# Three padding tiles in a two-layer encoder kernel: every fp32r operand of TensorE moves to a multiple of 128 bytes

## The chip, the cores and the metric

The kernel is one program for one core of a Trainium2 chip. The metric is device time in microseconds (us): the median of several executions, lower is better.

## What is computed

The reference is a trunk of two encoder layers over 1,024 tokens of 1,024 channels, in float32:

```
for l in range(2):
    h = rmsnorm(x) * (1 + sc1) + sh1
    proj = h @ w_in[l]                       # 1024 -> 5792 columns
    ya = latent attention(cq, ckv, kr)       # 8 heads, keys of 64 + 32 rope
    yb = pooling branch(pu); yc = gated convolution branch(cx, cb, cc)
    merged = sigmoid gates of (ya, yb, yc)
    x = x + g1 * (merged @ w_out[l])
    h2 = rmsnorm(x) * (1 + sc2) + sh2
    x = x + g2 * expert_choice_moe(h2)       # 16 experts, 128 tokens each, 1024 -> 1024 -> 1024
return rmsnorm(x)
```

## The kernel before

Every large product is worked out three times over. An operand is split in a high part (`hi`, rounded to the fp32r type) and a rest (`lo`), by ScalarE and VectorE in `split` (L110), and TensorE adds hi by hi, hi by lo and lo by hi (`mm3`, L320):

```
for i, (a, b) in enumerate(((w_hi, h_hi), (w_hi, h_lo), (w_lo, h_hi))):
    for q in range(n):
        s = slice(512 * q, 512 * q + 512)
        PE.matmul(dst[:, s], a, b[:, s], start=start and i == 0, stop=stop and i == 2)
```

In each matmul the first operand (`a`, 128 columns) is loaded into the array as weights, and the second (`b`, mostly 512 columns) streams through it; below they are the loaded and the streamed operand. Every matmul has a weight load of its own.

A layer runs through these stages, in the order of the program, with nothing that reorders it:

- the projections: `hhi`/`hlo` (the normalised input, transposed) stream past columns of weights `whi`/`wlo`. In between `yhi`/`ylo` stream past the convolution's output weights, and the sums of the modulation are taken. The first block is done by quarters of 256 columns (L485).
- attention: queries (`cqhi`/`cqlo` past `qw`), scores (`khi`/`klo` past a tile named `raw`, which holds the queries), softmax on VectorE and ScalarE, transposes (L859), and the values (L867, L869, 256 columns).
- merge (`ohi`/`olo`) and output projection (L1137, 256 columns, `rg` and `whi`/`wlo` past `rg`), with the router behind it.
- the experts: the 128 rows of an expert, transposed (`T00`, `T01`, `T10`, `T11`), are loaded, and the weights `whi`/`wlo` of 512 columns stream. SyncE fetches 1 MB pieces of the weights ahead into 16 buffers (L1035); ScalarE and VectorE split each piece; TensorE multiplies it.
- in the first layer, the last expert's rows are added by TensorE at the start of the second (L1512: `T10`/`T11` stream past a selection matrix that lies in a tile named `xg`).

Tiles lie in pools that are stacked from the left and from the right end of the scratch memory in the order in which they are opened, so where a tile begins follows from the sizes of all that were opened before it on its side:

```
consts = ctx.enter_context(tc.tile_pool(name="consts", bufs=1, side="left"))
small = ctx.enter_context(tc.tile_pool(name="small", bufs=4, side="left"))
self.pool = self.stack.enter_context(pool("W", bufs=2, side="left"))
Hp = hs.enter_context(pool("H", side="right"))
r = [ep.tile([128, 8, 128], F32R, name=f"T{e % 2}{i}", bufs=1) for i in range(2)]
```

Of the kernel before, what the change touches and what calls it, by code (L numbers as in the profile page):

```python
# [9 lines left out]
F32 = mybir.dt.float32  # L10
# [28 lines left out]
# chunks of the modulation worked out in turn between the projections of a layer  # L39
# [15 lines left out]
def encoder(ctx, tc, x, c, positions, w_mod, b_mod, norm1_g, w_in, b_gate, q_norm_g, w_uq, kv_norm_g,  # L55
# [17 lines left out]
    dram = ctx.enter_context(tc.tile_pool(name="scratch", bufs=1, space=DR))  # L73
    pstate = {}

    def psum_open(n2, n1):
        """n2 tiles of two banks, n1 of one"""
        if "stack" in pstate:
            pstate["stack"].close()
        pstate["stack"] = ExitStack()  # L80
        pstate["pool"] = pstate["stack"].enter_context(pool("psum", space=PS))
        pstate["n"] = (n2, n1)
# [7 lines left out]
    class Weights:  # L90
        """tiles of the weights: as loaded, and in two parts"""
# [8 lines left out]

    W = Weights()
# [10 lines left out]
    def behind(*ins):  # L112
        """what follows comes after these on their engines"""
        st = ExitStack()
        for i in ins:
            st.enter_context(tc.issue_after(i.ins))
        return st

    def gated(ins, by):
        """ins waits for by"""  # L120
        tc.add_manual_dep(ins.ins, by.ins.name, mybir.DependencyInfo(mybir.DependencyClass.Sync, mybir.DependencyReason.DATA),
                          reason="order")

    # ---------------------------------------------------------------- scratch in DRAM
# [10 lines left out]
    # ---------------------------------------------------------------- constants  # L135
# [26 lines left out]
    # row k, column p: one where k < p  # L162
# [15 lines left out]
    # every token's number in two parts, and its affinities in three  # L178
# [12 lines left out]
    # ---------------------------------------------------------------- modulation rows  # L191
# [7 lines left out]
    def mod_first(j, P_, crep, onec):  # L199
        """the same by the tensor engine alone, four parts of the sum side by side"""  # L200
        raw = mod_load(0, j, P_, 2 if P_ is W else 3)
        if j % 2 == 0:
            pend["pm"] = ps1()
        pm = pend["pm"]
        o = 256 * (j % 2)
        for k in range(8):
            g = k % 4
            PE.matmul(pm[32 * g:32 * g + 32, o:o + 256], crep[:, k, :], raw[:, k, :], start=(k < 4), stop=(k >= 4),
                      tile_position=(0, 32 * g))
        if j % 2 == 1:  # L210
            mp = pend["pool"].tile([128, 512], F32, name="mp", bufs=1)
            ACT.copy(mp, pm)
            pr = ps1()
            for i in range(4):
                PE.matmul(pr[:, i:i + 1], mp[:, 128 * i:128 * i + 128], onec, start=True, stop=True)
            DVE.tensor_copy(modT[:, 2 * (j - 1):2 * (j - 1) + 4], pr[:, 0:4])

    def mod_chunk(l, j):
        """256 of the modulation's columns: the sum over k on the vector engine; mod_sum() follows later"""
        raw = mod_load(l, j, W, 2)  # L220
        acc = pend["pool"].tile([128, 256], F32, name="macc", bufs=9)
        DVE.tensor_scalar(acc, raw[:, 0], csil[:, 0:1], None, op0=OP.mult)
        for k in range(1, 8):
            DVE.scalar_tensor_tensor(acc, raw[:, k], csil[:, k:k + 1], acc, op0=OP.mult, op1=OP.add)
        mod_sums.append((l, j, acc))

    def mod_sum(pending=0):
        """the sums over the partitions of four such chunks, side by side"""
# [14 lines left out]
    # chunks of the rows: sh1 0-3, sc1 4-7, g1 8-11, sh2 12-15, sc2 16-19, g2 20-23  # L243
# [51 lines left out]
    # ---------------------------------------------------------------- helpers  # L295
# [9 lines left out]
    def load_split(src, kt, cols, raw_eng=None):  # L305
        """[128, kt, cols] block of weights, split in two parts."""
        raw = W.tile([128, kt, cols], F32, name="raw", tag="raw")
        SP.dma_start(raw, src)
        hi = W.tile([128, kt, cols], F32R, name="whi", tag="whi")
        lo = W.tile([128, kt, cols], F32R, name="wlo", tag="wlo")  # L310
        split(hi, lo, raw)
        return hi, lo

    def mm3(dst, w_hi, w_lo, h_hi, h_lo, start, stop):
        """dst[:, half] += w.T @ h for both halves of 512 columns, w: [K,128], h: [K,1024]"""
# [6 lines left out]
    for l in range(DEPTH):  # L322
        x_in = x.rearrange("b s d -> (b s) d") if l == 0 else xres[l - 1]

        # ------------------------------------------------------------ vectors of the layer
# [15 lines left out]
        # ------------------------------------------------------------ h, transposed, in two parts  # L341
# [23 lines left out]
        def block():  # L365
            """the next block of weights; the one after it is fetched meanwhile"""
            fetch()
            return ready.pop(0)
# [19 lines left out]
        if l == 0:  # L388
            psum_open(2, 4)
            with pool("xt", side="right") as xp:  # L390
# [9 lines left out]
                def hx_half(t, hf):  # L400
                    """half of the rows' columns, transposed"""
# [75 lines left out]
        def proj_quarters(dsts, w):  # L477
            """two column blocks, a quarter of the tokens after the other"""
# [21 lines left out]
        # ------------------------------------------------------------ gated convolution branch  # L500
# [66 lines left out]
        # ------------------------------------------------------------ pooling branch  # L567
# [63 lines left out]
        # ------------------------------------------------------------ gains of the norms  # L631
        def gain(pp, i, l_):
            """one plus the scale, times the norm's weights, as rows of 128"""
# [8 lines left out]
        # ------------------------------------------------------------ low-rank queries, keys and values  # L642
# [13 lines left out]
        with pool("cqt", side="left") as cp:  # L656
# [38 lines left out]
            # rope part of the keys: columns and the same columns with their halves swapped, both parts side by side  # L695
# [27 lines left out]
            def prepare(pp):  # L723
                # the router's weights with the norm's gain in them, and what the shift adds to its logits
# [23 lines left out]
            for dp in range(4):  # L748
                wg = block()
                for d in (2 * dp, 2 * dp + 1):  # L750
# [7 lines left out]
                    # w_out with the gate g1 of the residual in it  # L758
# [13 lines left out]
        # ------------------------------------------------------------ attention  # L772
        with pool("att", side="right") as ap:
# [27 lines left out]
            def k_pair(hp):  # L801
                """keys of two heads, and the query weights of both"""
# [60 lines left out]
            def av(h, g, phi, plo, po):  # L863
                """two query tiles, g = 0..3; po is [128, 512] for two g"""
# [85 lines left out]
        # ------------------------------------------------------------ merge and output projection  # L950
# [6 lines left out]
        # gated sum, transposed: [half of the tokens][part][half of the channels]  # L957
# [14 lines left out]
        def wout_load(q):  # L972
            """a quarter of w_out's columns, with the gate g1 of the residual in it"""
# [41 lines left out]
        def slot(s_):  # L1015
            """a buffer of two rows of k of an expert's weights"""
            p_, tag, bufs = s_
            return p_.tile([128, 2, 1024], F32, name="rg", tag=tag, bufs=bufs)
# [9 lines left out]
        def prefetch(n, by=None):  # L1028
            for _ in range(n):
                if chunks:  # L1030
                    w, e, j = chunks.pop(0)
                    # the last ones leave the buffers outside the ring to the rows of x
# [8 lines left out]
        with pool("wout", side="left") as op_:  # L1041
# [4 lines left out]
            # the 128 largest so far, the ranks of each eight reversed, and a copy for the steps of the merge  # L1046
# [8 lines left out]
            def top_round(i, r):  # L1055
                """eight more of a list's sorted 128 largest, in blocks from the last"""
# [5 lines left out]
            def merged(i):  # L1062
                """a list's largest into the largest so far"""
# [7 lines left out]
            def sort_steps(src, d0, d1, steps, rev):  # L1071
                """the steps of a merge, to d0 and d1 in turn"""
# [11 lines left out]
            def copied(t, dst, src):  # L1084
                """the last tile's copies stay off the scalar engine, which is busy then"""
                (ACT.copy if t < 7 else DVE.tensor_copy)(dst, src)

            def quick_sort(t):
                """a tile's affinities, sorted by 32 in four places, of which two with the sign turned"""
# [25 lines left out]
            def quick_list(t):  # L1115
                """the four merged: from the smallest by eights; the very last tile's stay unsorted by twos"""
# [75 lines left out]
            def h2_rows(t):  # L1192
                """the normalised rows, to be gathered by the experts"""
# [90 lines left out]
            # the 128th largest of every expert, on all partitions  # L1284
# [8 lines left out]
            # the tokens above it and those equal to it, each counted in their order  # L1293
# [22 lines left out]
        # ------------------------------------------------------------ experts  # L1316
# [3 lines left out]
        if True:  # L1320
# [40 lines left out]

            hot, idx, val, pick = {}, {}, {}, {}
            choose_last, gathers = [None], []

            def choose(e):
                """a one in the row of a token and the column of its slot"""
# [10 lines left out]
            def chosen(e):  # L1377
                """token and affinity of every slot"""
# [47 lines left out]
            for e in range(E):  # L1426
# [13 lines left out]
                if e + 2 == E:  # L1440
                    if not last:
                        # the first weights of the next layer
                        pend["w0"] = ring.tile([128, 8, 256], F32, name="rg", tag="rg", bufs=N_RING)
                        SP.dma_start(pend["w0"], cols(w_in[l + 1], O_CX, 256))
                    # the last expert's rows are added on chip
# [4 lines left out]
                    if last:  # L1450
                        # their rows as they are before it
# [11 lines left out]
                    # what the next norm multiplies by and adds  # L1463
# [6 lines left out]
            if last:  # L1470
                # the rows without the last expert's, then its rows over them
# [34 lines left out]
            def last_rows(t, xt, sel, ys):  # L1506
                """the last expert's rows onto 128 tokens"""
# [47 lines left out]
```

## Time and profile before

| | |
|---|---|
| three runs | 3419.47, 3422.6, 3423.29 us; median 3422.6 |
| span of the profiled execution | 3420.4 us (first to last instruction; its time outside the span is not listed) |
| TensorE busy | 3232.3 us, 94% of the span, 16,593 matmuls |
| VectorE, ScalarE, GpSimd busy | 2443.6, 1856.7, 384.1 us |
| mean granted clock of TensorE | 0.973 |
| moved by DMA | 686 MB, 201 GB/s |

A busy share is an average over stages with different limits, and matmuls overlap in the records: one that streams 512 columns is listed at some 395 ns, while the next one starts about 230 ns after it. So times between starts are what count, and the timeline shows them: a row of the timeline joins neighbouring instructions of one kind, and from the start of one row to the start of a later one, divided by the matmuls in between, is the time that one matmul takes up.

### The profile page before, as it was taken

The numbers are of one execution on the slowest core, as the hardware profiler recorded it, in microseconds if no ns is written. First come the engines' busy times: TensorE is split into PE (matmuls) and PEld (weight loads), VectorE is DVE, ScalarE is ACT, GpSimd is POOL, SyncE is SP. The second block draws the span as 40 slices with busy tenths as digits, with TensorE's granted clock in tenths as the row PEclk, the third lists the DMA queues.
The fourth block names the chain that finished last, engine by engine and source line by source line (L and its number), as shares of the span: only waits on it lengthen the run. The fifth ranks groups of instructions, "written<-read, shape, count | busy, mean of one in ns | idle before, by whom it ended". The sixth has DMA issues, their size and how long they took to land.

```text
span 3420.4 us, 43057 instructions
## 1 busy us (share of the span) xinstructions
PE 3232.3 (94%) x16593; PEld 2670.8 (78%) x16593; DVE 2443.6 (71%) x3730; ACT 1856.7 (54%) x2535; POOL 384.1 (11%) x364
## 2 busy tenths in 40 slices
PE   6999999999978799999989999999999869999996
PEld 5787787788878688888778887777887868888875
DVE  5555525499848899999864345347997488999997
ACT  5111213488734788887631121226885348888876
POOL 2001011000034101001020000010001330101010
PEclk8999999999989899999999999999999879999998
DMA  6346334100355899999622344340004559999994
GB/s 219 117 148 206 109 122 132 64 17 7 129 189 203 300 390 381 387 390 371 246 61 78 131 156 136 101 160 24 14 34 160 202 188 356 380 388 378 392 377 180
DMA packets 283373, 686.00 MB, mean 201 GB/s; under 512 B 24934, under 2 KB 139840, under 8 KB 283168
## 3 DMA queue, kind: packets, MB, share of 16 engines
q1 hardware_dynamic: 247008, 563.13, 44.4%
q0 software_dynamic: 33856, 111.74, 10.3%
q10 hardware_dynamic: 2304, 8.39, 0.7%
q8 instruction: 130, 2.13, 0.3%
q14 instruction: 75, 0.61, 0.1%
HBM read 607.63 MB, written 75.55 MB: 200 GB/s over the span
## 4 chain that ended last, share of the span: by engine, by line
PE 77%; DVE 12%; ACT 4%; DMA 3%; issue 2%; POOL 1%; SPq 0%; POOLq 0%; ACTq 0%; DVEq 0%
PE ps L320 63%; PE pa L1137 3%; DVE wlo L110 3%; PE pa L320 3%; DVE mx L841 2%; PE pa L859 2%; PE ps L1346 1%; DMA gh<-gate 1%; PE pa L867 1%; PE pa L869 1%; ACT pexp L846 1%; ACT whi L110 1%; DVE af L1060 1%; DVE top L1058 1%; PE pa L1178 1%
## 5 line engine op out<-in xcount | busy, mean ns | idle before, releaser
L110 DVE TENSOR_TENSOR wlo<-rg,whi 128x1024 fp32r<-128x1024 f32 x768 | 899.8, 1220 | 99.7 <-ACT whi L110 96.8
L110 ACT CAST whi<-rg 128x1024 fp32r<-128x1024 f32 x768 | 762.1, 1045 | 184.3 <-PE ps L320 184.2
L320 PE MATMUL ps<-whi,T 128*128 128x512 f32 x3072 | 846.9, 395 | 4.5 <-DVE T L110 2.3
L320 PEld LDWEIGHTS ps<-whi,T 128*128 128x128 f32 x3072 | 575.3, 189 | 130.5 <-DVE T L110 3.2
L320 PE MATMUL ps<-wlo,T 128*128 128x512 f32 x1536 | 490.7, 401 | 4.5 <-DVE wlo L110 2.5
L320 PE MATMUL ps<-hhi,whi 128*128 128x512 f32 x1376 | 437.1, 399 | 0.0
L320 PE MATMUL ps<-hlo,whi 128*128 128x512 f32 x1376 | 433.9, 396 | 0.0
L320 PE MATMUL ps<-hhi,wlo 128*128 128x512 f32 x1376 | 433.9, 396 | 0.0
L320 PEld LDWEIGHTS ps<-wlo,T 128*128 128x128 f32 x1536 | 281.1, 189 | 71.9 <-DVE wlo L110 14.6
L110 ACT CAST whi<-raw 128x2048 fp32r<-128x2048 f32 (+2 forms) x59 | 101.0, 1713 | 430.5 <-PE ps L320 409.2
L320 PEld LDWEIGHTS ps<-hhi,whi 128*128 128x128 f32 x1376 | 257.7, 188 | 67.6 <-issue 4.2
L320 PEld LDWEIGHTS ps<-hhi,wlo 128*128 128x128 f32 x1376 | 259.2, 188 | 63.2
L320 PEld LDWEIGHTS ps<-hlo,whi 128*128 128x128 f32 x1376 | 259.1, 188 | 63.1
L1137 PE MATMUL pa<-rg 128*128 128x256 f32 x768 | 189.4, 301 | 30.0 <-DVE rg L110 13.9
L110 DVE TENSOR_TENSOR wlo<-raw,whi 128x2048 fp32r<-128x2048 f32 (+2 forms) x59 | 121.0, 2051 | 107.9 <-ACT whi L110 107.9
L320 PE MATMUL ps<-khi,raw 128*128 128x512 f32 x512 | 167.2, 407 | 7.0 <-ACT pexp L846 5.7
L1137 PEld LDWEIGHTS pa<-rg 128*128 128x128 f32 x768 | 146.2, 203 | 33.2 <-DVE rg L110 15.0
L110 DVE TENSOR_TENSOR wlo<-pa,whi 128x512 fp32r<-128x512 f32 x256 | 169.5, 681 | 1.3 <-ACT whi L110 1.0
L1437 POOL DMA_INDIRECT xres<-y,idx x30 | 72.3, 2411 | 780.8 <-DVE y L1436 780.8
L846 ACT ACTIVATE pexp<-ps,nm 128x1024 f32<-128x1024 f32 x128 | 143.1, 1118 | 29.7 <-DVE nm L843 26.7
L841 DVE TENSOR_REDUCE mx<-ps 128x1 f32<-128x1024 f32 x128 | 155.1, 1213 | 5.5 <-PE ps L320 4.5
L110 ACT CAST whi<-pa 128x512 fp32r<-128x512 f32 x256 | 139.6, 588 | 8.4 <-PE pa L859 7.5
(409 smaller groups left out, 4894.8 us busy)
## 6 DMA issues: line engine op xcount, KB each, us to landing
rg<-in_w_gate_dram SPq DMA_DIRECT2D x128, 1024.0 KB, 9.3
rg<-in_w_up_dram SPq DMA_DIRECT2D x128, 1024.0 KB, 7.1
rg<-in_w_down_dram SPq DMA_DIRECT2D x128, 1024.0 KB, 7.9
raw<-in_w_mod_dram SPq DMA_DIRECT2D x48, 1024.0 KB, 5.4
raw<-in_w_in_dram SPq DMA_DIRECT2D x43, 1024.0 KB, 5.2
part<-pr POOLq DMA_DIRECT2D x32, 512.0 KB, 3.7
pr<-part POOLq DMA_DIRECT2D x16, 512.0 KB, 4.4
sq<-in_w_out_dram POOLq DMA_DIRECT2D x16, 512.0 KB, 4.5
```

Source lines behind the costliest of these rows:

```text
L110: return ACT.copy(hi, src), DVE.tensor_sub(lo, src, f(hi))
L320: PE.matmul(dst[:, s], a, b[:, s], start=start and i == 0, stop=stop and i == 2)
L841: DVE.reduce_max(mx, p, axis=AX.X)
L846: ACT.activation(e, p, AF.Exp, bias=nm, scale=SCALE, accum_out=sm)
L859: PE.transpose(p[:, 128 * k:128 * k + 128], e[:, o:o + 128], ident)
L867: PE.matmul(po[:, o:o + 256], vt[:, k, h, :], phi[:, k, :], start=(k == 0), stop=False, skip_group_check=True)
L869: PE.matmul(po[0:64, o:o + 256], vt[:, k, h, 0:64], plo[:, k, :], start=False, stop=(k == 7), skip_group_check=True)
L1058: DVE.max(v[:, 15 - r, :], a)
L1060: DVE.match_replace(a, v[:, 15 - r, :], a, -1.0)
L1137: PE.matmul(p[q // 2][:, 256 * (q % 2):256 * (q % 2) + 256], a, wos[q][b][:, k, :], skip_group_check=True, start=(k == 0 and i == 0 and q ...
L1178: PE.matmul(pls[t][:, :E], hT[:, 128 * k:128 * k + 128], wra[:, kk, :], start=(kk == 0), stop=(kk == 7))
L1437: POOL.indirect_dma_start(out=xres[l], in_=y, in_offset=None, compute_op=OP.add, out_offset=bass.IndirectOffsetOnAxis(ap=idx[e][:, 0:1], a ...
```

## The change

Three small tiles that nothing reads or writes are put in: 96 bytes per partition at the right end, 64 bytes on the left behind the constants, and 64 bytes in the pool of the experts, ahead of the `T` tiles. All other lines of the difference are comments.

```
@@ -71,10 +71,13 @@
     small = ctx.enter_context(tc.tile_pool(name="small", bufs=4, side="left"))
     dram = ctx.enter_context(tc.tile_pool(name="scratch", bufs=1, space=DR))
+
+    edge = ctx.enter_context(tc.tile_pool(name="edge", bufs=1, side="right"))
+    edge.tile([128, 24], F32, name="edge")
     pstate = {}
...
+    edge = ctx.enter_context(tc.tile_pool(name="edge2", bufs=1, side="left"))
+    edge.tile([128, 16], F32, name="edge2")
     W = Weights()
     W.open()
...
             hot, idx, val, pick = {}, {}, {}, {}
+            ep.tile([128, 16], F32, name="phase")
             choose_last, gathers = [None], []
```

No instruction is added, removed or moved: the lists of the five engines are the same row for row, with the same waits, 9,513 rows on TensorE's. What differs is where operands begin. In bytes past a multiple of 128, from the two built programs, for the 13,888 matmuls with fp32r operands:

| matmuls | streamed, loaded operand | columns | number | before (streamed, loaded) | after |
|---|---|---|---|---|---|
| projections, L320 | `hhi`/`hlo`, `whi`/`wlo` | 512 | 4,128 | 96, 64 | 0, 0 |
| keys' rope part, L705 | `hhi`/`hlo`, `rk` | 512 | 64 | 96, 64 | 0, 0 |
| first block, L485 | `hhi`/`hlo`, `whi`/`wlo` | 256 | 384 | 96, 64 | 0, 0 |
| scores, L320 | `khi`/`klo`, `raw` | 512 | 768 | 96, 64 | 0, 0 |
| queries, L320 | `cqhi`/`cqlo`, `qw` | 512 | 288 | 64, 96 | 0, 0 |
| values, L867 and L869 | `whi`/`wlo`, `vt` | 256 | 1,024 | 64, 96 | 0, 0 |
| output projection, L1137 | `rg`, `rg` | 256 | 768 | 96, 96 | 0, 0 |
| output projection, L1137 | `whi`/`wlo`, `rg` | 256 | 768 | 64, 96 | 0, 0 |
| experts, L320 | `whi`/`wlo`, `T00` to `T11` | 512 | 4,608 | 64, 0 | 0, 0 |
| `y`, `o`, `m` and `ck` products, L320 | `yhi`, `ohi`, `mhi`, `ckhi`, ... | 512 | 1,056 | 64, 64 | 0, 0 |
| last expert's rows, L1512 | `T10`/`T11`, `xg` | 512 | 32 | 0, 0 | 0, 0 |

The matmuls with plain float32 operands (transposes, sums) mostly move to 0 too; 64 of the 128 at the start (L208) have their loaded operand `crep` moved from 64 to 96.

## Rows read from the trace of the kernel before

**Rows 1.** The page: the chain that ended last, by engine and by line.

```profile
PE 77%; DVE 12%; ACT 4%; DMA 3%; issue 2%; POOL 1%; SPq 0%; POOLq 0%; ACTq 0%; DVEq 0%
PE ps L320 63%; PE pa L1137 3%; DVE wlo L110 3%; PE pa L320 3%; DVE mx L841 2%; PE pa L859 2%; PE ps L1346 1%; DMA gh<-gate 1%; PE pa L867 1%; PE pa L869 1%; ACT pexp L846 1%; ACT whi L110 1%; DVE af L1060 1%; DVE top L1058 1%; PE pa L1178 1%
```

**Rows 2.** Windows: length, busy PE, PEld, DVE, ACT, POOL; clock, DMA share, GB/s.

```profile
80.00:600.00 520.00, 520.00 (x2249) 412.71 (x2249) 266.95 (x357) 107.81 (x86) 41.80 (x78) 1.00 0.43 140
640.00:900.00 260.00, 253.83 (x1555) 217.96 (x1555) 237.66 (x469) 215.86 (x396) 1.60 (x3) 1.00 0.07 25
...
1150.00:1660.00 510.00, 508.54 (x2394) 411.64 (x2393) 470.90 (x445) 421.07 (x504) 48.96 (x28) 1.00 1.02 380
```

**Rows 3.** Timeline of TensorE in the projections (start, length; 26th row is last).

```profile
570.61 0.64 PE L320 MATMUL ps<-hhi,whi 128*128 128x512 f32 x2
...
582.33 0.63 PE L320 MATMUL ps<-hlo,whi 128*128 128x512 f32 x2
```

**Rows 4.** Timeline in the convolution's output product (22nd row is last).

```profile
251.44 0.61 PE L320 MATMUL ps<-yhi,wlo 128*128 128x512 f32 x2
...
260.96 0.61 PE L320 MATMUL ps<-yhi,wlo 128*128 128x512 f32 x2
```

**Rows 5.** Timeline in the last product of layer one's experts (7th row is last).

```profile
1704.81 1.07 PE L320 MATMUL ps<-whi,T 128*128 128x512 f32 x4
...
1708.93 1.07 PE L320 MATMUL ps<-whi,T 128*128 128x512 f32 x4
```

**Rows 6.** Timeline where the last expert's rows are added, four matmuls and what follows.

```profile
1728.89 1.07 PE L1512 MATMUL pa<-T,xg 128*128 128x512 f32 x4
1729.80 0.60 PE L385 MATMUL pa<-ident,xn 128*128 128x128 f32 x4
```

**Rows 7.** Timeline in the queries' product (11th row is last).

```profile
712.76 0.40 PE L320 MATMUL pa<-cqlo,qw 128*128 128x512 f32 x1
...
716.26 0.40 PE L320 MATMUL pa<-cqlo,qw 128*128 128x512 f32 x1
```

**Rows 8.** Groups of matmuls by operands: count, busy us, mean ns.

```profile
L320 PE MATMUL ps<-whi,T 128*128 128x512 f32 x3072 | 846.9, 395 | 4.5 <-DVE T L110 2.3 <-ACT T L110 2.2
...
L320 PE MATMUL ps<-hhi,whi 128*128 128x512 f32 x1376 | 437.1, 399 | 0.0
...
L320 PE MATMUL ps<-khi,raw 128*128 128x512 f32 x512 | 167.2, 407 | 7.0 <-ACT pexp L846 5.7 <-ACT raw L110 1.3
...
L320 PE MATMUL pa<-cqhi,qw 128*128 128x512 f32 x192 | 62.8, 394 | 3.0 <-ACT qw L110 3.0
```

**Rows 9.** Chain of attention in layer one (690 to 900 us), by line.

```profile
by line: PE ps L320 15.9%; PE pa L320 15.7%; DVE mx L841 12.7%; PE pa L859 10.9%; DVE wlo L110 8.0%; PE pa L867 7.1%; PE pa L869 6.8%; ACT pexp L846 6.1%; DVE pexp L849 3.6%; ACT whi L110 2.1%; DVE op L879 1.9%; DVE raw L110 1.7%; ACT ohi L
```

**Rows 10.** Timeline in the output projection (16th row is last).

```profile
1047.29 0.29 PE L1137 MATMUL pa<-rg 128*128 128x256 f32 x1
...
1049.08 0.28 PE L1137 MATMUL pa<-whi,rg 128*128 128x256 f32 x1
```

**Rows 11.** Timeline in the values (13th row is last).

```profile
688.73 0.28 PE L869 MATMUL pa<-wlo,vt 128*64 128x256 f32 x1
...
690.13 0.28 PE L869 MATMUL pa<-wlo,vt 128*64 128x256 f32 x1
```

**Rows 12.** Waits in the experts (1300 to 1600 us): total, times, longest.

```profile
ACT whi L110 <- PE ps L320: 41.2, 57, 1.2
```

**Rows 13.** Waits of SyncE's queue in the experts (1150 to 1710 us).

```profile
SPq L1035 <- DVE wlo L110: 378.4, 145, 5.2
```

**Rows 14.** Timeline of four matmuls of L1512 at half clock, and what follows.

```profile
1741.27 1.91 PE L1512 MATMUL pa<-T,xg 128*128 128x512 f32 x4
1742.98 0.41 PE L385 MATMUL pa<-ident,xn 128*128 128x128 f32 x1
```

**Rows 15.** Two stretches of L1512: the clock granted (PEclk).

```profile
1741.30:1742.90 1.60, 1.60 (x5) 1.19 (x5) 1.28 (x3) 1.54 (x4) 0.32 (x1) 0.50 0.04 15
1728.90:1729.80 0.90, 0.90 (x6) 0.69 (x5) 0.90 (x3) 0.87 (x2) 0.11 (x1) 1.00 0.00 0
```

More of the change, by code (lines that the diff above doesn't have):

```diff
@@ L73, in encoder @@
     dram = ctx.enter_context(tc.tile_pool(name="scratch", bufs=1, space=DR))
+    edge = ctx.enter_context(tc.tile_pool(name="edge", bufs=1, side="right"))
+    edge.tile([128, 24], F32, name="edge")
     pstate = {}
@@ L99, in close @@
             self.stack.close()
+    edge = ctx.enter_context(tc.tile_pool(name="edge2", bufs=1, side="left"))
+    edge.tile([128, 16], F32, name="edge2")
     W = Weights()
@@ L1362, in encoder @@
             hot, idx, val, pick = {}, {}, {}, {}
+            ep.tile([128, 16], F32, name="phase")
             choose_last, gathers = [None], []
```

## The prediction

> **What bounds the kernel now.** I read the page first, then the busy times of three stretches, the chain of waits, and last the timeline of TensorE. TensorE holds 77% of the chain that ends last, and the line of the split products, L320, 63% of the whole span [rows 1]. In the projections TensorE is busy without a gap, VectorE for 267 of 520 us; in the experts TensorE for 508.5 of 510 us, VectorE for 470.9; only in attention are TensorE (253.8 of 260) and VectorE (237.7) close to each other [rows 2]. In the experts ScalarE waits for TensorE to give a buffer back [rows 12], and the queue that fetches the weights waits for buffers too, 378 us in all [rows 13]; so neither the splits nor the loads hold TensorE up there. A matmul that takes up less time therefore shortens projections and experts one for one.
>
> The next question is how long a matmul takes up, from start to start, and whether that goes with where its operands begin (the offsets are those of the table in the change; here as streamed, loaded). The projections (96, 64): from 570.61 to 582.33 lie 25 rows of two matmuls, 11.72 us / 50 = **234.4 ns** [rows 3]. The convolution's output (64, 64), same line of code, same 512 columns, same stage: 21 rows of two, 9.52 us / 42 = **226.7 ns** [rows 4]. The experts (64, 0): 18 matmuls in 4.12 us, **228.9 ns** [rows 5]. The queries (64, 96): 15 in 3.50 us, **233.3 ns** [rows 7]. So the two kinds with a 96 in them stand near 234, the two without at 227 to 229. One small group already has what the change gives to all, (0, 0): the rows of the last expert, four matmuls at full clock [rows 15] from 1728.89 to the next row at 1729.80, 0.91 us / 4 = **227.5 ns** [rows 6]. That is the floor of (64, 64), on few samples.
>
> What else could make the difference? Not the load of the other engines: the 226.7 and the 234.4 stand in the same stage, with VectorE half idle [rows 2]. Not the clock, which is full in all of these stretches [rows 2]. What is left is the offset, or something else about the place of the tiles that goes with it.
>
> **The change part by part.** It issues nothing and moves nothing, so no wait, queue or DMA is added; the three tiles cost space alone. Each term is a number of matmuls by the difference of two such times.
>
> 1. *Projections and the keys' rope part*, 4,128 + 64 matmuls of (96, 64); the 4,128 are three groups of 1,376 [rows 8]. From 234.4 to 226.7 ns: 4,192 x 7.7 = **32.3 us**, all on the path, since TensorE has no gap there.
> 2. *Experts*, 3,072 [rows 8] and half as many with `wlo`, 4,608 of (64, 0). From 228.9 to 226.7: 4,608 x 2.2 = **10.1 us**, on the path. VectorE is the cover that could run out: it is busy for 470.9 of 510 us, so there are 39 us to take from TensorE in a layer before it leads, and the term takes 5.
> 3. *Scores and queries in attention*: 512 [rows 8] and half as many with `klo`, 768 of (96, 64), for which I take the projections' step, 768 x 7.7 = 5.9 us; 192 [rows 8] and half as many with `cqlo`, 288 of (64, 96), 288 x 6.6 = 1.9 us. Together 7.8, of which I count TensorE's share of the chain there, 15.9 + 15.7 + 10.9 + 7.1 + 6.8 = 56% [rows 9]: **4.4 us**. VectorE and ScalarE, late next, keep the rest.
> 4. *Matmuls of 256 columns*: 1,536 in the output projection at 1.79 us / 15 = 119.3 ns [rows 10], 1,024 in the values at 1.40 us / 12 = 116.7 [rows 11], 384 at the start (taken at 119 too). No row shows one at (0, 0). From below, half of a full-rate 512 (next paragraph), 106.7 ns: 2,944 x some 11.5 = 34 us, about half on the path, so 17. From above, the highest of these classes, 119.3, for the values too: 1,024 x 2.6 = 2.7 us lost. They are far apart, and the rows themselves hardly differ between offsets, so I take **0**.
> 5. *The 1,056 of (64, 64) and 32 of (0, 0)*: at the floor already, **0**. The float32 matmuls, `crep` among them, and the operands of the other engines and of the DMAs begin elsewhere too; no row prices that. The 128 matmuls with `crep`, should half of them lose the 7.7 ns that 96 costs above, cost 0.5 us; taken as 0.
>
> How low could (0, 0) go? At half clock, 1.2 GHz [rows 15], four matmuls of L1512 take 1742.98 - 1741.27 = 1.71 us, 427 ns each [rows 14], which is 512 columns at one per cycle and nothing else. At 2.4 GHz that would be 213.3 ns. It is the lower bound of every term above, and the same group at the same offsets did not reach it [rows 6]; so 226.7, the row that its 227.5 is nearest to, is taken.
>
> Sum: 32.3 + 10.1 + 4.4 = 46.8 us. The profiled span is 3420.4 us; the three runs' median, 3422.6, is 2.2 us above it, within their own spread of 3.8. Taken off the span it gives 3373.6 us, off the median **3375.8 us**, 1.4% less.
>
> A rule that speaks against all this: the Trainium skill, "TensorE: Matmul & The Clock Gate", section "Step-by-step: what each phase is for", says that TensorE has two independent read ports to the scratch memory, one for what streams and one for the weights, so that loading the next weights takes nothing from the running matmul; and its "Back-to-back issue gap" gives N columns over the clock plus 2.5 ns, 216 ns for 512, with no term for an address. By it all five kinds above would stand at 216 whatever their offsets, and the change would do nothing: the sum would be 0 and the time 3422.6 us. The trace does not agree with the 216: nothing here is below 226.7, and kinds of the same shape differ by 8 ns.
>
> **Rivals.**
> - *The offset is not the cause* (bank, size of the tile or something else of the place, which moves by at most 128 bytes): nothing changes, **3422.6 us**. For it: each level belongs to a pair of tiles, and there are few pairs. Against it: two kinds with a 96, in different stages and with different tiles, stand at 233 to 234, and three without at 227 to 229 [rows 3 to 7]. The Trainium skill's rule of two ports, weighed above, would end here.
> - *(0, 0) streams at full rate*, 213.3 ns. Then 4,192 x 21.1 = 88.5 and 4,608 x 15.6 = 71.9 (36 a layer, just within VectorE's 39), the 1,056 give 1,056 x 13.4 = 14.2, attention (768 x 21.1 + 288 x 20) x 56% = 12.3, and 256 columns 17: 204 us less, **some 3219 us**. Against it: [rows 6].
> - *The other side: 64 is the good offset of what streams, and 0 is as bad as 96.* In all large kinds at 227 to 229 the streamed operand is at 64. Then the projections stay, the experts go from 228.9 to 234.4, 4,608 x 5.5 = +25.3 us, and the 1,056 pay 7.7 each, +8.1: **3456 us**, slower. It decides if (0, 0) takes more than about 231.5 ns in common, where 4,192 x 2.9 = 12.2 gained is 4,608 x 2.6 = 12.0 lost. Against it: again the 227.5 of [rows 6].
> - *Only the 96 counts*: the experts stay at 228.9, and the time is 3375.8 + 10.1 = **3386 us**. For it: 64 and 0 may both be good, and the experts' 2 ns be due to something else.
>
> **How the numbers follow.** My forecast, 72%; only the 96 counts, 10%; no change, 7%; full rate, 6%; 0 as bad as 96, 5%. The forecast's own range is 3358 to 3388: below, term 4 may give its 17 us; above, attention may give nothing, the experts half, and term 4 lose its 2.7. With the rival of the 96 alone, and some way to the others on either side (a spacing of 224 ns would take another 24 us), the range is 3348 to 3402. A difference under 0.2%, 7 us, is about what a measurement of this kernel can't tell from no change. Faster: 72 + 10 + 6 = 88%; same 7%; slower 5%.
>
> **What would show it.** In the profile after: the projections' timeline at 11.3 us for 50 matmuls where it was 11.72; the experts' at 4.08 us for 18; the convolution's output still 9.52 for 42; the same numbers of matmuls, and the clock as before. In the busy times of the groups, `hhi` and `yhi` matmuls equally long. I am wrong if projections stay at 234 (not the offset), if they fall towards 213 (full rate), or if the experts rise above 229; and if both fall as said and the time does not, another engine took the gain, to be looked for in VectorE's waits in experts and attention.

## The result, and the profile after

The changed kernel takes 3386.5 us (median of four runs, 3384.2 to 3389.8), the kernel before 3422.5 (four runs beside them, 3419.5 to 3423.3): a ratio of 0.9897, 95% interval 0.9884 to 0.9911. It is 36.0 us faster; 46.8 were forecast. The profiled execution has a span of 3386.5 us (before 3420.4) at a mean granted clock of 0.971 (0.973), with 16,593 matmuls as before.

The page after: busy time of each engine, and the chain that ended last by engine and by line. Line numbers are 5 to 7 higher than before: the split products stand in L325, `split` in L115.

```profile
PE 3201.4 (95%) x16593; PEld 2672.0 (79%) x16593; DVE 2442.3 (72%) x3730; ACT 1857.7 (55%) x2535; POOL 384.2 (11%) x364
...
PE 77%; DVE 12%; ACT 4%; DMA 3%; issue 2%; POOL 1%; SPq 0%; POOLq 0%; DVEq 0%; ACTq 0%
PE ps L325 62%; PE pa L1142 4%; DVE wlo L115 3%; PE pa L325 2%; DVE mx L846 2%; PE pa L864 2%; PE ps L1351 1%; PE pa L872 1%; PE pa L874 1%; DMA gh<-gate 1%; ACT pexp L851 1%; ACT whi L115 1%; DVE af L1065 1%; PE pa L1183 1%; DVE top L1063 1%
```

The chain is made up as in [rows 1]; no engine has taken TensorE's place in it. The windows of the same three stages say the same beside [rows 2] (columns as there):

```profile
80.00:590.00 510.00, 510.00 (x2263) 414.52 (x2262) 267.35 (x358) 107.68 (x87) 43.27 (x81) 1.00 0.44 146
630.00:890.00 260.00, 254.45 (x1574) 220.07 (x1572) 238.89 (x471) 217.10 (x394) 1.60 (x3) 0.99 0.07 25
1130.00:1640.00 510.00, 508.38 (x2407) 412.38 (x2407) 468.63 (x447) 424.69 (x507) 49.03 (x28) 1.00 1.02 381
```

In the projections 2,263 matmuls now fall into 510 us where 2,249 fell into 520. In the experts it is only 2,407 for 2,394 in the same 510 us.

The timeline of TensorE after, in the projections, which answers to [rows 3] (the 26th row is last):

```profile
560.43 0.61 PE L325 MATMUL ps<-hhi,whi 128*128 128x512 f32 x2
...
571.77 0.62 PE L325 MATMUL ps<-hlo,whi 128*128 128x512 f32 x2
```

50 matmuls in 11.34 us are 226.8 ns each; they were 234.4. In the convolution's output product, [rows 4] (the 20th row is last):

```profile
245.92 0.61 PE L325 MATMUL ps<-ylo,whi 128*128 128x512 f32 x2
...
254.53 0.61 PE L325 MATMUL ps<-yhi,wlo 128*128 128x512 f32 x2
```

38 in 8.61 us, 226.6 ns, as before. In the last product of layer one's experts, [rows 5] (the 7th row is last):

```profile
1688.22 1.07 PE L325 MATMUL ps<-whi,T 128*128 128x512 f32 x4
...
1692.30 1.07 PE L325 MATMUL ps<-whi,T 128*128 128x512 f32 x4
```

18 in 4.08 us, 226.7 ns (before 228.9). And in the queries, [rows 7] (the 11th row is last):

```profile
697.99 0.62 PE L325 MATMUL pa<-cqhi,qw 128*128 128x512 f32 x2
...
701.42 0.39 PE L325 MATMUL pa<-cqhi,qw 128*128 128x512 f32 x1
```

15 in 3.43 us, 228.7 ns; they were 233.3 and have not come down to 226.7.

Where the 34.0 us of the span came from, in us: the first matmul of a stage to the first of the next, after less before, layer one and layer two. It is one profiled execution of each kernel.

| stage | layer 1 | layer 2 | both | predicted |
|---|---|---|---|---|
| first block of 256 columns | -1.30 | +0.40 | -0.90 | 0 |
| projections, with the rest of L325 there | -12.05 | -12.38 | -24.43 | -32.3 with the next row |
| keys' rope part and what of the projections follows it | -2.94 | -2.94 | -5.88 | |
| attention | +0.67 | -2.46 | -1.79 | -4.4 |
| merge | +0.64 | -0.59 | +0.05 | 0 |
| output projection, router | +0.26 | +0.39 | +0.65 | 0 |
| experts | -1.94 | -0.41 | -2.35 | -10.1 |

The stages left out give +0.7.

Projections and rope part give 30.3 us of the forecast's 32.3. In this pair of traces the experts give a quarter of what was expected, attention less than half.

### The profile page after: what moved, and what is told of

It reads as the page before. It is cut to its first block, busy times and chain, and to the rows that moved or that the text cites. A ratio compares the mean times of both kernels' runs of the same rounds, so it can differ in the third digit from the quotient of the medians.

```text
span 3386.5 us, 43057 instructions
## 1 busy us (share of the span) xinstructions
PE 3201.4 (95%) x16593; PEld 2672.0 (79%) x16593; DVE 2442.3 (72%) x3730; ACT 1857.7 (55%) x2535; POOL 384.2 (11%) x364
## 4 chain that ended last, share of the span: by engine, by line
PE 77%; DVE 12%; ACT 4%; DMA 3%; issue 2%; POOL 1%; SPq 0%; POOLq 0%; DVEq 0%; ACTq 0%
PE ps L325 62%; PE pa L1142 4%; DVE wlo L115 3%; PE pa L325 2%; DVE mx L846 2%; PE pa L864 2%; PE ps L1351 1%; PE pa L872 1%; PE pa L874 1%; DMA gh<-gate 1%; ACT pexp L851 1%; ACT whi L115 1%; DVE af L1065 1%; PE pa L1183 1%; DVE top L1063 1%
## 5 line engine op out<-in xcount | busy, mean ns | idle before, releaser
L115 DVE TENSOR_TENSOR wlo<-rg,whi 128x1024 fp32r<-128x1024 f32 x768 | 899.5, 1219 | 99.2 <-ACT whi L115 95.7
L115 ACT CAST whi<-rg 128x1024 fp32r<-128x1024 f32 x768 | 763.8, 1048 | 181.0 <-PE ps L325 181.0
L325 PE MATMUL ps<-whi,T 128*128 128x512 f32 x3072 | 841.8, 393 | 4.0 <-ACT T L115 2.2
L325 PEld LDWEIGHTS ps<-whi,T 128*128 128x128 f32 x3072 | 574.8, 189 | 126.4 <-ACT T L115 3.1
L325 PE MATMUL ps<-wlo,T 128*128 128x512 f32 x1536 | 489.1, 400 | 5.0 <-DVE wlo L115 3.0
L325 PE MATMUL ps<-hhi,whi 128*128 128x512 f32 x1376 | 427.4, 392 | 0.0
L325 PE MATMUL ps<-hlo,whi 128*128 128x512 f32 x1376 | 423.9, 389 | 0.0
L325 PE MATMUL ps<-hhi,wlo 128*128 128x512 f32 x1376 | 423.8, 389 | 0.0
L325 PEld LDWEIGHTS ps<-wlo,T 128*128 128x128 f32 x1536 | 281.3, 189 | 74.3 <-DVE wlo L115 19.0
L115 ACT CAST whi<-raw 128x2048 fp32r<-128x2048 f32 (+2 forms) x59 | 101.1, 1713 | 417.1 <-PE ps L325 360.8
L325 PEld LDWEIGHTS ps<-hhi,whi 128*128 128x128 f32 x1376 | 256.9, 188 | 58.9 <-issue 4.2
L325 PEld LDWEIGHTS ps<-hlo,whi 128*128 128x128 f32 x1376 | 258.3, 188 | 54.1
L325 PEld LDWEIGHTS ps<-hhi,wlo 128*128 128x128 f32 x1376 | 258.3, 188 | 54.0
L1142 PE MATMUL pa<-rg 128*128 128x256 f32 x768 | 191.4, 304 | 28.1 <-DVE rg L115 13.4
L115 DVE TENSOR_TENSOR wlo<-raw,whi 128x2048 fp32r<-128x2048 f32 (+2 forms) x59 | 120.9, 2050 | 98.5 <-ACT whi L115 98.5
L325 PE MATMUL ps<-khi,raw 128*128 128x512 f32 x512 | 166.5, 406 | 7.2 <-ACT pexp L851 5.7
L115 DVE TENSOR_TENSOR wlo<-pa,whi 128x512 fp32r<-128x512 f32 x256 | 169.3, 680 | 1.3 <-ACT whi L115 1.1
L115 ACT CAST whi<-pa 128x512 fp32r<-128x512 f32 x256 | 139.6, 588 | 7.6 <-PE pa L864 6.5
```

The costliest lines, as they stand in the source:

```text
L115: return ACT.copy(hi, src), DVE.tensor_sub(lo, src, f(hi))
L1142: PE.matmul(p[q // 2][:, 256 * (q % 2):256 * (q % 2) + 256], a, wos[q][b][:, k, :], skip_group_check=True, start=(k == 0 and i == 0 and q ...
```

## What was tried

**Which offsets make a matmul short?** The prediction took the offsets modulo 128 as such: 0 and 64 short, 96 long. The trace of before allows a second reading. Where both operands begin at the same offset, (64, 64) and (0, 0), a matmul took 227; where they differ it took 229 to 234. So there were two theories: L, the level of each operand by itself, and P, the pair: what counts is that both begin at the same offset. Four kernels tell them apart. They differ in the padding alone. The offsets in what follows are past a multiple of 512 bytes, so that distances over 128 can be told apart; before, `hhi` begins at 480 and `whi` at 320, after the change both at 384.

*right*: of the three tiles `edge` alone is kept (diff against the changed kernel). Projections stand at 384 and 320, the experts as before.

```
-    edge = ctx.enter_context(tc.tile_pool(name="edge2", bufs=1, side="left"))
-    edge.tile([128, 16], F32, name="edge2")
...
-            ep.tile([128, 16], F32, name="phase")
```

> Only the 96 bytes at the right end are kept, so the projections go from (96, 64) to (0, 64), streamed and loaded, queries and values to (64, 0), and the experts stay at (64, 0). Theory P, that the difference between the two offsets counts (0: 226.7 ns per 512 columns, 64: 228.9, 32 or 96: 233 to 234): projections at 228.9, some 22 us less than before, 3400 us. Theory L, that each operand counts by itself and only a 96 costs: projections at 226.7, some 32 us less, 3390 us.

Measured: 3397.3 us, ratio 0.9927 (0.9910 to 0.9944). The timeline of its projections (the 26th row is last):

```profile
561.02 0.62 PE L323 MATMUL ps<-hhi,wlo 128*128 128x512 f32 x2
...
572.47 0.62 PE L323 MATMUL ps<-hhi,whi 128*128 128x512 f32 x2
```

50 in 11.45 us: 229.0 ns, the level that the experts had before at the same distance of 64, and not 226.7. That speaks for P.

*left*: the other two tiles alone. Projections at 480 and 384, experts both at 384.

```
-    edge = ctx.enter_context(tc.tile_pool(name="edge", bufs=1, side="right"))
-    edge.tile([128, 24], F32, name="edge")
```

> Only the two tiles on the left are kept: projections at (96, 0), experts and the y, o, m and ck products at (0, 0). Theory P: a difference of 96, as the queries had before, 233.3 ns in the projections, some 4 us less, and the experts' 2.4 us, 3416 us. Theory L: the 96 costs what it cost, 234.4 ns, 3420 us.

Measured: 3413.4 us, ratio 0.9976 (0.9966 to 0.9986); projections at 233.4 ns, which is P's 233.3 rather than L's 234.4, and experts at 227.9.

*all64* and *all96*: every operand at 64, or at 96, past a multiple of 128, by other sizes of the tiles (all64 above the dots, all96 below; these diffs and those that follow are against the changed kernel).

```
-    edge.tile([128, 24], F32, name="edge")
+    edge.tile([128, 8], F32, name="edge")
-    edge = ctx.enter_context(tc.tile_pool(name="edge2", bufs=1, side="left"))
-    edge.tile([128, 16], F32, name="edge2")
...
-    edge = ctx.enter_context(tc.tile_pool(name="edge", bufs=1, side="right"))
-    edge.tile([128, 24], F32, name="edge")
-    edge.tile([128, 16], F32, name="edge2")
+    edge.tile([128, 8], F32, name="edge2")
```

> Every fp32r operand begins 64 bytes past a multiple of 128, (64, 64) throughout. Theories P and L both: 226.7 ns in projections and experts, 3386.5 us as with the change. If it is the multiple of 128 that counts, projections above 226.7 and a time towards 3422.

> Every fp32r operand begins 96 bytes past a multiple of 128, (96, 96) throughout. Theory P: difference 0, 226.7 ns everywhere, 3386.5 us as with the change. Theory L: 234 ns everywhere, the experts (4608 x 5.5 = 25 us) and the 1056 of (64, 64) (8 us) slower than before, 3455 us.

Measured: 3406.2 us, ratio 0.9962 (0.9948 to 0.9976), and 3408.0 us, 0.9962 (0.9947 to 0.9976). Neither theory had these. The experts came to 227.8 and 227.9 ns in both, at 64 as at 96, so a 96 is not long in itself, and L falls. But the projections did not follow. The timeline of all64's projections (the 11th row is last):

```profile
567.04 0.62 PE L323 MATMUL ps<-hhi,wlo 128*128 128x512 f32 x2
...
571.68 0.64 PE L323 MATMUL ps<-hhi,whi 128*128 128x512 f32 x2
```

20 in 4.64 us are 232.0 ns. What sets the projections apart from the experts in these two kernels is seen only past 128: `hhi` at 448 and `whi` at 320 in all64, 480 and 352 in all96. Equal modulo 128, they are 128 bytes apart, while the experts' operands are 0 apart. So P was mended to Q: the distance counts modulo something over 128, taken to be 512; and M was put beside it, that both must begin at a multiple of 128, as the change has it.

*same352*: `hhi`, `whi` and `T` at 352, the scores' `khi` at 96 (256 from its `raw`), no fp32r operand at a multiple of 128. *apart256*: all at multiples of 128, `hhi` at 128 and `whi` at 384 (same352 above the dots).

```
-    edge.tile([128, 24], F32, name="edge")
+    edge.tile([128, 32], F32, name="edge")
-    edge.tile([128, 16], F32, name="edge2")
+    edge.tile([128, 8], F32, name="edge2")
...
-    edge.tile([128, 24], F32, name="edge")
+    edge.tile([128, 88], F32, name="edge")
```

> Every operand of projections, experts and output projection begins 352 bytes past a multiple of 512, so 96 past a multiple of 128, and streamed and loaded operand are 0 apart modulo 512. Theory Q, that the distance between the two modulo 512 counts (0: 226.7 ns, 64: 228.9, the others seen 232 to 234): 226.7 in projections and experts, 3386.5 us as with the change. Theory M, that both must begin at a multiple of 128: projections at 232 as with all at 96, 3408 us.

> The right end is padded by 352 bytes in place of 96: every operand begins at a multiple of 128, but the projections' streamed operand lies 256 from the loaded one modulo 512 (scores and values lie 0 apart instead). Theory Q: projections at 231 to 234 ns, 18 to 30 us of the gain lost, 3405 to 3415 us. Theory M: 226.7 ns, 3386.5 us.

Measured: same352 3388.1 us, ratio 0.9905 (0.9889 to 0.9922); apart256 3384.6 us, 0.9892 (0.9875 to 0.9908). The timelines of their projections, same352 first (in both the 26th row is last):

```profile
559.90 0.61 PE L325 MATMUL ps<-hhi,wlo 128*128 128x512 f32 x2
...
571.23 0.62 PE L325 MATMUL ps<-hhi,whi 128*128 128x512 f32 x2
```

```profile
559.73 0.61 PE L325 MATMUL ps<-hlo,whi 128*128 128x512 f32 x2
...
571.06 0.62 PE L325 MATMUL ps<-hhi,wlo 128*128 128x512 f32 x2
```

11.33 us for 50 in each, 226.6 ns. A kernel without one fp32r operand at a multiple of 128 has the whole gain: M's "must" falls. And 256 apart is as good as 0: Q's 512 falls too. That leaves Q', the distance modulo 256.

*apart128*: all at multiples of 128, `hhi` at 256 and `whi` at 384. *apart32* and *apart192*: `hhi` at 416 and at 320, one execution each.

```
-    edge.tile([128, 24], F32, name="edge")
+    edge.tile([128, 56], F32, name="edge")
```

(16 and 40 in place of 56 for the other two.)

> The padding on the right is 224 bytes instead of 96, so that every fp32r operand still begins at a multiple of 128 bytes, but streamed and loaded operands of the projections, scores and values lie 128 bytes apart modulo 256 (256 and 384 past a multiple of 512). Theory M, a multiple of 128 for both operands is what makes a matmul short: projections at 226.7 ns from start to start, 3386.5 us. Theory Q', what counts is the distance of the two operands modulo 256 bytes: projections at about 232.4 ns as in all64 and all96, their three stretches some 9 us a layer longer than after the change, scores a little longer too, 3405 to 3410 us.

> The padding on the right is 64 bytes: streamed and loaded operands of the projections 32 bytes apart modulo 256. Theory M: no multiple of 128, so it should be at 229 to 234 ns. Theory Q': no distance under 64 has been seen; between 226.7 (distance 0) and 229.0 (distance 64), about 228, some 3390 us.

> The padding on the right is 160 bytes: streamed and loaded operands of the projections 192 bytes apart modulo 256, which is 64 on the other side. Theory M: as apart32. Theory Q' with a distance that counts in both directions alike: 229.0 ns as at 64, some 3396 us; with one that counts upwards only: above the 234.4 of distance 160, some 3420 us.

Measured: apart128 3406.3 us, ratio 0.9957 (0.9940 to 0.9974). The timeline of its projections (the 21st row is last):

```profile
563.13 0.62 PE L325 MATMUL ps<-hlo,whi 128*128 128x512 f32 x2
...
572.43 0.62 PE L325 MATMUL ps<-hhi,whi 128*128 128x512 f32 x2
```

40 in 9.30 us, 232.5 ns, as Q' had it: with every fp32r operand at a multiple of 128, 20 of the 36 us are gone. The words of the change are neither needed (same352) nor enough (apart128). The other two, 3412.4 and 3411.3 us, both with projections at 233.3 ns, missed what Q' had guessed from its neighbours (3390; 3396 or 3420): 32 is not between 0 and 64, and 192 is neither like 64 nor above 160.

The kernels together. A distance is streamed less loaded operand, modulo 256; the ns are means from the start of a matmul to the next start over the whole trace, worked out from the start times of all records at full clock, with those of 260 ns and more left out, 4,098 in the projections and some 4,390 in the experts. Each kernel's time was taken beside one of the kernel before, which stood at 3420.7 to 3422.5 us.

| kernel | projections: distance, ns | experts: distance, ns | us |
|---|---|---|---|
| before | 160, 234.2 | 64, 229.4 | 3422.5 |
| after | 0, 226.9 | 0, 227.9 | 3386.5 |
| same352 | 0, 226.9 | 0, 227.9 | 3388.1 |
| apart256 | 0, 226.9 | 0, 227.8 | 3384.6 |
| nophase (below) | 0, 226.9 | 64, 229.4 | 3391.3 |
| apart32 | 32, 233.3 | 0, 227.9 | 3412.4 |
| right | 64, 229.0 | 64, 229.5 | 3397.3 |
| left | 96, 233.4 | 0, 227.9 | 3413.4 |
| all64 | 128, 232.6 | 0, 227.8 | 3406.2 |
| all96 | 128, 232.6 | 0, 227.9 | 3408.0 |
| apart128 | 128, 232.7 | 0, 227.8 | 3406.3 |
| apart192 | 192, 233.3 | 0, 227.9 | 3411.3 |

At 0 and at 128, the distances that several kernels have, the level in the projections is the same to 0.1 ns, whatever the offsets themselves. The queries, other tiles in another stage, go by it too: 233.2 ns at 96 (before), 233.2 at 192 (right), 233.7 at 224 (apart32), but 229.9 at 64 (apart192) and 229.2 at 0 (after).

The distance can also be seen at work inside one kernel. 48 of the projections' 4,128 matmuls have their weights at other places, 128 bytes further off modulo 256 than the rest. In the kernel after, six at 128 alternate there with six at 0 (the six from 517.85 are at 128, the six from 519.24 at 0):

```profile
517.85 0.64 PE L325 MATMUL ps<-hhi,whi 128*128 128x512 f32 x2
...
519.24 0.62 PE L325 MATMUL ps<-hhi,whi 128*128 128x512 f32 x2
...
520.61 0.64 PE L325 MATMUL ps<-hhi,whi 128*128 128x512 f32 x2
```

1.39 and 1.37 us for six, 232 and 228 ns each. Over all such places of the kernel after, those at 128 take 232.6 ns on average (46 of them), the neighbours at 0 229.3 (36); in all64, where the two change places, those at 0 take 228.0 (46) and the neighbours at 128 232.8 (36). So it isn't something else in which whole kernels differ. Whether a matmul's own weights count or those of the next one, which here nearly always lie at the same distance, isn't settled.

Matmuls of 256 columns do not follow this order. The first block has the operands of the projections; its matmuls take 119.6 to 119.8 ns at 0 (four kernels), 119.8 at 96 (left), 118.0 at 160 (before), 117.3 at 64 (right) and 116.3 at 192 (apart192). The values take 117.0 at 0, 117.7 at 64 (apart192) and 115.4 at 192 (right). So 192 is the shortest for both, and for the first block 0 is among the longest.

**Where did the experts' gain go?** Two theories: D, that VectorE, which splits the weights, came too late more often and held the matmuls up; S, that they lose their gain at the interruptions themselves. For D speak TensorE's waits for the splits in layer one's experts, before and then after (total us, times, longest):

```profile
PEld ps L320 <- DVE wlo L110: 7.8, 14, 1.1
```

```profile
PEld ps L325 <- DVE wlo L115: 10.0, 26, 1.1
```

*half_before* and *half_after* leave out every second low part of the experts' weights, in the kernel before and in the changed one: the matmuls run as before, with the first piece's `lo` in its place.

```
-                            split(hi[:, kk], lo[:, kk], raw[:, kk])
+                            if kk == 0:
+                                split(hi[:, kk], lo[:, kk], raw[:, kk])
+                            else:
+                                ACT.copy(hi[:, kk], raw[:, kk])
...
-                        mm3(p, aT[0][:, k, :], aT[1][:, k, :], hi[:, kk], lo[:, kk], k == 0, k == 7)
+                        mm3(p, aT[0][:, k, :], aT[1][:, k, :], hi[:, kk], lo[:, kk if anchors is not None else 0], k == 0, k == 7)
```

> The kernel before, with every second split of the experts' weights without its low part (the product takes the neighbour's, so the low parts are wrong): VectorE has half of that work, TensorE all of its own. It is the yardstick for the next run: experts at most 1153 us for both layers together, the kernel before's.

> The same left out of the changed kernel. Theory D, that in the experts TensorE now meets splits that come late, so the gain is given back in waits for VectorE: with VectorE relieved the experts of both layers are 10 us shorter than in the run before this one, the whole term. Theory S, that TensorE itself is slow for some matmuls after each interruption, whatever VectorE does: shorter by 2 to 5 us only, as in the full kernels (1153.1 against 1150.7).

Measured (one execution each): 3409.6 and 3379.0 us. The window of half_after in the experts, columns as in [rows 2]:

```profile
1150.00:1650.00 500.00, 497.21 (x2362) 406.04 (x2361) 279.14 (x268) 412.53 (x490) 36.58 (x27) 1.00 1.00 379
```

VectorE is down to 279 of 500 us. Both layers' experts take 1144.7 us in half_before and 1141.6 in half_after, 8.4 and 9.1 less than with all splits. With VectorE out of the way the change gives the experts 3.1 us, not 10: D falls as the whole explanation. It does not fall altogether. In their experts half_after stood at half clock for 10.7 us, half_before for 5.1 (in the table below). At half clock four matmuls took 427 ns each [rows 14], so by estimate the clock hides up to half of the difference, 2.8 us, and without it the gain could be 5.9 us; in the full kernels, at half clock for 13.0 and 10.8 us, it could be 3.4 in the same way. That late splits take up to 2.5 us is therefore not ruled out.

*nophase*: the change without its third tile. The experts' distance is 64 again, the rest as after. (The tile also moves what lies behind it in its pool, `xg`, `sg` and `both`; in all64 these lie where nophase has them.)

```
-            ep.tile([128, 16], F32, name="phase")
```

> The change without its third tile: only the T tiles of the experts move, 64 bytes back, so that the experts' operands are 64 apart modulo 256 and everything else is as after the change. By the sizes of the prediction's term 2 the experts take 10.1 us more than after the change: 3396.6 us. Theory S, with matmuls that need a run of undisturbed ones to settle to 226.7 and so win less than the steady spacing says: experts 2.4 us longer (what their stretches gained), 3389 us.

Measured: 3391.3 us, ratio 0.9910 (0.9894 to 0.9927); its experts take 1155.7 us, 5.0 more than after. That is nearer to S than to the 10.1 of term 2, and between the two; by the time alone nophase and the kernel after can't be told apart, since their intervals overlap. What the experts' time is made of, both layers, in us, summed from start to start by kind, with the time at half clock from the trace's record of the granted clock:

| | before | after | nophase | all64 | half_before | half_after |
|---|---|---|---|---|---|---|
| mean of the undisturbed matmuls, ns | 229.4 | 227.9 | 229.4 | 227.8 | 229.4 | 227.6 |
| from start to start 260 ns and more | 84.7 | 85.3 | 90.1 | 78.9 | 65.9 | 68.9 |
| transposes of `xg` | 24.0 | 26.5 | 24.3 | 26.2 | 25.1 | 27.1 |
| transposes of `sg` | 28.1 | 28.1 | 28.1 | 28.1 | 28.1 | 28.1 |
| `tv` past `both` | 9.5 | 11.0 | 9.5 | 10.9 | 7.6 | 8.5 |
| of the whole, at half clock | 10.8 | 13.0 | 20.9 | 4.9 | 5.1 | 10.7 |

The undisturbed matmuls give 4,388 x 1.53 = 6.7 us. The short matmuls that break into them take 2.5 + 1.5 = 4.0 us back. One such place, the first two transposes of `xg` for an expert, in the timelines of before, after and nophase:

```profile
1327.04 0.38 PE L1346 MATMUL ps<-ident,xg 128*128 128x128 f32 x2
1327.25 0.73 PE L320 MATMUL ps<-wlo,T 128*128 128x512 f32 x2
```

```profile
1312.74 0.38 PE L1351 MATMUL ps<-ident,xg 128*128 128x128 f32 x2
1313.05 0.73 PE L325 MATMUL ps<-wlo,T 128*128 128x512 f32 x2
```

```profile
1315.11 0.38 PE L1351 MATMUL ps<-ident,xg 128*128 128x128 f32 x2
1315.32 0.73 PE L325 MATMUL ps<-wlo,T 128*128 128x512 f32 x2
```

From the transposes to the next `wlo` it is 0.21 us at a distance of 64 and 0.31 at 0. It goes with the distance of the experts' own operands: all64 has `xg` and `both` where nophase has them, and yet the longer times. It isn't only VectorE either, since half_after has it too (27.1 for 25.1). Why a better distance makes these gaps longer is open. By this account the distance alone is worth 6.5 - 2.2 - 1.4 = 2.9 us between nophase and after. The rest of the 5.0 lies in the row of 260 ns and more, which holds not only waits but also the matmuls at half clock. The ends of layer one's experts in nophase and in the kernel after (the last but two figures are the clock):

```profile
1680.00:1692.00 12.00, 9.31 (x31) 6.57 (x30) 6.75 (x6) 4.63 (x5) 0.00 (x0) 0.72 0.85 344
1675.00:1690.00 15.00, 11.43 (x52) 8.77 (x51) 10.57 (x11) 8.14 (x9) 0.00 (x0) 1.00 0.72 281
```

In both kernels TensorE had just waited 1.32 us for `sg` and 1.10 us for `T` there; in nophase the clock then fell to 1.2 GHz at 1684.8 us, in the kernel after it stayed at 2.4. In both layers together nophase stood at half clock for 20.9 us and the kernel after for 13.0; by estimate up to half of the difference, 4.0 us, comes from that, so the clock can account for the rest. All twelve kernels of the table above point the same way: the experts take 1153.1 to 1155.7 us in the three at a distance of 64 and 1146.9 to 1150.7 in the nine at 0, 5.3 apart in the mean; but the three also stood longer at half clock (15.8 us in the mean, the nine 9.8). With half of the time at half clock taken off each, 2.3 us are left between the means.

## Why the prediction was right, and where its sizes were off

The mechanism held: nothing was moved, a matmul that is shorter from start to start shortens projections one for one, and VectorE did not become the bound. The time lies in the range, and in the forecast's own, 10.7 us above its number. The rule from which it was forecast was wrong, and luck had a part: by that rule apart128, with every operand at a multiple of 128, would take 3375.8 us too, and it took 3406.3. The padding chosen happens to make nearly all distances 0 modulo 256.

1. *Projections and rope part*: predicted 4,192 x 7.7 = 32.3, measured 30.3. The two rows of one stretch each, 234.4 and 226.7, were a little far apart: over all of them it is 234.2 and 226.9, 4,192 x 7.3 = 30.6.
2. *Experts*: predicted 10.1, measured 2.35 in this pair of traces, and in the means over all kernels 5.3, or 2.3 with the clock taken out by estimate. This is the term that was mis-sized. The level 226.7 was right for a long undisturbed stretch, in which [rows 5] and the row after were both read; but an expert is broken five times, by `xg`, `sg` and `tv`, and in the kernel after the first ten undisturbed matmuls behind a break or wait take 227 to 233 ns in the mean, place by place, before all stand at 226.7. So the mean fell by 1.5 ns, not 2.2, and the breaks became 4.0 us longer, a cost that the prediction did not have at all. Its own cover, VectorE's 39 us in a layer, was not what took most of it; whether late splits took up to 2.5 us stays open.
3. *Attention*: predicted 4.4, measured 1.8. The fault lies in the steps taken: the scores come in runs of six matmuls between transposes and never settle: 233.9 to 230.5 ns, not 226.7; the queries 233.2 to 229.2. 768 x 3.4 + 288 x 4.0 = 3.8 us, and 56% of it are 2.1. That the share of the chain was right isn't shown by this: the two layers, +0.67 and -2.46, differ by more than the term.
4. *256 columns*: predicted 0, measured -0.9 in the first block and +0.65 in the output projection, whose matmuls went from a mean of 119.1 ns to 119.6; the values stood at 117. The first block's own matmuls became longer, 118.0 to 119.8, so its 0.9 are not theirs. These matmuls do depend on the place, by 3.5 ns between the kernels in the first block, but in another order than those of 512 columns.
5. *(64, 64) and (0, 0)*: nothing, as predicted; `yhi` 226.6 for 226.7.

The reason given was half right. That the offsets are the cause is shown: the rival without them would have kept 3422.6. But "0 and 64 good, 96 bad" was a reading of the wrong variable; it happened to order the rows of before rightly, because there (96, 64), (64, 96) and (64, 0) were at distances 160, 96 and 64, and (64, 64) and (0, 0) at 0. "(0, 0) at full rate" is out, at 226.9. "0 as bad as 96" is out. "Only the 96 counts" gave 3386 us, the number measured; it is right by accident, since all96 has experts at 227.9 with both operands at 96, and apart128 projections at 232.7 with no 96 in them. The rule weighed in the prediction, the Trainium skill, "TensorE: Matmul & The Clock Gate", section "Back-to-back issue gap", has no term for an address and would have kept 3422.6 us. The section calls its 216 ns the gap of an isolated matmul and gives some 131 ns for streams of weight loads and matmuls, which the prediction left out. The runs differ from both: the addresses alone moved the projections from 234.2 to 226.9 ns, and 226.9 is the lowest mean in the table of the kernels.

## What to carry to other kernels

Look at the pair, not at the alignment: where matmuls follow each other back to back, lay the streamed and the loaded tile so that their starts differ by a multiple of 256 bytes (here 7 ns of 234 for the fp32r ones of 512 columns), whether or not either start is a round number. For another number of columns measure it anew: with 256 columns it was 192 bytes that gave the shortest matmuls here. When several kinds of one instruction differ in time, list every simple function of their addresses that orders them alike, and run the one kernel that tells these apart. And price a faster steady state only for the stretches that are long enough to be in it: count the breaks, and read the first rows behind one.

## What the runs showed of the hardware that was not expected

- The time of an fp32r matmul of 512 columns with its own weight load goes by the distance of its two operands modulo 256 bytes, and not smoothly: 226.9 ns at 0, 229.0 at 64, 232.6 at 128, and 233.3 to 234.2 at 32, 96, 160 and 192. Distances that are no multiple of 32 weren't tried, and why it is so is open.
- It has a direction: with the streamed operand's start 64 bytes above the loaded one's a matmul took 229.0 ns, with 192, which is 64 below, 233.3.
- At 256 columns the order is another: in the first block 116.3 ns at 192, 117.3 at 64, 119.7 at 0.
- At distance 0 the experts' matmuls need ten places behind a break or wait to settle at 226.7 ns, and the breaks are dearer: 0.31 us for two small transposes where 64 has 0.21.
